# A planner's duration for a TensorE product, taken from the trace

## The chip, the cores and the metric

The kernel runs on one core of a Trainium2 chip. The core has five engines that run side by side, each with its own queue in program order: TensorE (PE, matrix products into PSUM; PEld is its weight load), VectorE (DVE), ScalarE (ACT), GpSimd (POOL) and SyncE (SP, which only issues transfers). An engine waits at a semaphore till an operand of its next instruction is ready, and what stands behind that instruction waits with it. The metric is the device time of one execution in microseconds (us); lower is better.

## The reference, cut to what matters

Two layers of a decoder trunk for 2048 prompt tokens and 8 sample tokens of width 1024, in float32:

```python
# layer 0
p = rms_norm(x) @ w_in                      # 1024 -> 3592
glu_val, glu_gate, gate_a, qkv, z, beta, a = split(p)
c = silu(layer_norm(causal_conv31(glu_val * sigmoid(glu_gate)))) * silu(gate_a)
q, k, v = silu(causal_conv4(qkv)); o = gated_delta_rule(l2(q), l2(k), v, g, beta)
x = x + concat(c, rms_norm(o) * silu(z)) @ w_out
x = x + softmax(rms_norm(x) @ wq @ k_mem.T / 16) @ v_mem @ wo
# layer 1
u, gate = split(rms_norm(x) @ w_in_odd)
x = x + ((mean_pool(u) - u) @ w_pool + b) * scale * silu(gate) @ w_out_odd
x = x + softmax(rms_norm(x) @ wq @ k_mem.T / 16) @ v_mem @ wo
y = rms_norm(x)
```

The sample tokens have memory keys and values of their own (caches of 256 rows for each token), and states for the convolutions, the delta rule and the pooling.

## The kernel before

Products are done in float32r: every operand is split into a high and a low part, and high x high, high x low and low x high are summed in a PSUM bank. An output block of 128 channels over a token tile is thus 24 products (3 pairs of parts x 8 groups of 128 input channels). Small products of side work are plain float32.

**Stages, in the order of the program.** Phase 1 makes the memory's keys and values, and then the input projection: 28 blocks of 128 channels over five token tiles (three of 512, two of 260). The blocks are ordered: four times a gate and a value block, with twelve q/k/v blocks between them, then two z blocks (2 and 3) and four sg blocks. A value block ends on DVE (`fin_val`, L222: glu <- glu, ps_mm). The long convolution (`conv31`) is 30 taps on DVE for each half of a channel block, each an operation cacc <- glu, dww, cacc over 1024 tokens, 240 in all; the short one (`conv4`) is three operations qacc on DVE after a scaled copy on ACT, and ahead of it DVE copies three columns (raw <- raw). `sample_mix` does the same for the sample tokens in many narrow steps on DVE with small products between them (ps_cs sums m_sq over the partitions; ps_ks and ps_vb belong to its delta rule, 8 times each). Phase 2 is the gated delta rule in 16 chunks (`prep`, `inv16`, `levels`, `scan`, `onorms`) beside dense products (`Fill`). Then come the output projection, the attention of layer 0, the pooling, the gated half of the odd layer, and the attention of layer 1. Beside these runs `sample_attn`, once for each layer: it reads each sample token's cached keys and values in blocks of [128, 512] over the queue of GpSimd into three places a_big, and DVE multiplies and sums each half of a block (L222: a_big <- a_big). For two such blocks there is one more load, of the query (d_sq) or the softmax weights (d_sp); this makes a round: one load of d_sq or d_sp, two blocks, four DVE operations. A layer has 32 rounds, 16 for keys and 16 for values.

**What sets the order.** Every operation is recorded through class `Flow`, which keeps a clock for each engine and for each tensor. An operation starts, by these clocks, when its engine and its operands are free, and lasts what a formula says: a product by `mm` (L160), an ACT operation by `act_cost`, a DVE operation with a per-partition factor 1/0.96 ns an element plus 130 ns (`stt`, up to L222). Dense work is a generator that yields after some four to twelve products; at each yield `pump` steps every side task whose time by the clocks has come (`item[1] <= t["pe"]`), unless DVE or ACT are by their clocks further ahead of PE than a limit (`LIM`, 1.5 to 3.8 us). `until` lets dense work stand still by the clocks till a condition holds. Some helpers choose ACT or DVE, or DVE or GpSimd, by the same clocks (`move`, `rows`, `ve`). Transfers join their queue when their data are ready by the clocks. No clock is measured: all this happens once, when the program is built, and the chip then runs each queue in the order that came out.

Of the kernel before, what the change touches and what calls it, by code (L numbers as in the profile page):

```python
# [30 lines left out]
class Pool:  # L31
    """A tile pool that notes whose place each tile takes."""
# [23 lines left out]
class Flow:  # L56
    """Engine wrappers that keep rough clocks of the engines and of the data, and the interleaving of side tasks with
    dense work by these clocks."""

    LIM = (1500.0, 3500.0, 1e9)  # L60
    # what passes from the end of an operation till another one sees its result
    VIS = {"pe": 130.0, "act": 190.0, "dve": 130.0, "pool": 110.0}

    def __init__(self, nc, tc):
        self.nc, self.tc = nc, tc
        self.rel = {}
        self.t = {"pe": 0.0, "act": 0.0, "dve": 0.0, "pool": 0.0, "sync": 0.0, "gpsimd": 0.0, "scalar": 0.0}
        self.hw = self.ring = 0.0
        self.tick, self.cold, self.cols = 0, True, 0.0
        self.cur = self.t0 = 0.0  # L70
        self.tasks = []
        # by tensor: writes and reads as (first, last partition, first, last element, time), last use, free place
        self.wr, self.rd, self.last, self.slot = {}, {}, {}, {}
        # stores that wait for their data before they join their queue: by tensor, time and arguments
        self.pend = {}
# [13 lines left out]
    def region(ap):  # L89
        a, o = ap.ap, ap.offset  # L90
        n = ap.tensor.name
        if ap.space == DRAM or a[0][0] == 0:
            # (writes to DRAM never meet earlier ones here)
            return n, -1, 1, o, o + sum((c - 1) * abs(s) for s, c in a)
# [12 lines left out]
    def ready(self, ins, outs, eng):  # L107
# [3 lines left out]
        for r in outs:  # L111
# [3 lines left out]
            # products on the same place of PSUM follow each other without a wait  # L115
# [32 lines left out]
    def pe_op(self, cost, out, lhsT, rhs):  # L148
        """the array's clock halves after a tick with too little work"""
# [10 lines left out]
    def mm(self, out, lhsT, rhs, start=True, stop=True, cost=None):  # L160
        n = fsz(rhs)
        if cost is None:
            cost = max(n, 248) * 0.422 if lhsT.dtype == F32R else max(n, 64) * 1.69
# [24 lines left out]
    def move(self, out, in_, scale=None):  # L188
        """copy on whichever of ScalarE and VectorE is free first"""
# [8 lines left out]
    def rows(self, out, in_, f):  # L198
        """out[:, h, :] = in_[:, h, :] * f[:, h], on whichever of ScalarE and VectorE ends first"""
# [7 lines left out]
    def ve(self, n, w=0.0):  # L207
        """VectorE or GpSimdE for an operation on n elements a partition, whichever ends first"""
# [55 lines left out]
    def dma(self, out, in_, eng="sync"):  # L264
        """a transfer; it joins its queue, where each waits for the ones before it, only when its data and place are ready"""
# [41 lines left out]
    def split(self, hi, lo, src, eng="dve", scale=1.0):  # L307
        """hi + lo == src, both in float32r."""
# [4 lines left out]
    def spawn(self, gen, hi=1, front=False):  # L313
        """hi: 2 what dense work waits for soon, 1 what it waits for later, 0 what may wait"""
# [34 lines left out]
    def until(self, cond):  # L349
        """dense work: let side tasks go on till cond holds"""  # L350
# [7 lines left out]
    def run(self, dense=None):  # L358
        """Alternate dense quanta (generator) with side-task steps until the dense work ends."""
# [42 lines left out]
def rsqrt(F, pool, y, x, n, tag, eng="dve"):  # L402
    """y = x ** -0.5 on a narrow float32 tile [128, n]."""
# [11 lines left out]
def token_rstd(F, C, pool, ppool, acc, n, scale, tag):  # L415
    """acc [128, n] holds partial sums; returns [128, nc] of (sum over partitions * scale + eps) ** -0.5,
    tokens on partitions."""
# [11 lines left out]
def spread(F, C, pool, ppool, r, n, tag, dg=None):  # L429
    """r [128, nc] tokens on partitions -> psum [128, n], every partition holding the row of tokens."""  # L430
# [15 lines left out]
def mm3_steps(F, out, K, w, x):  # L446
    """generator: out += (w0 + w1)^T (x0 + x1) without the product of the two low parts."""
# [21 lines left out]
class Ring:  # L469
    """Weight blocks [128, width] in two float32r parts, in n places that are taken in turn; they are loaded in parts of  # L470
    lw columns."""

    def __init__(self, F, pool, n, raw, width=1024, lw=512, tag="r"):
# [6 lines left out]
        # where the places lie, as [pool, number], and the ring that had the first ones  # L480
        self.where, self.prev = [[pool, n]], None
        # a second pool for the parts as they come, as (pool, number, up to which block)
# [6 lines left out]
    def has(self, name, i):  # L489
        """the block is in place by the clocks"""  # L490
# [10 lines left out]
    def place(self, i):  # L501
        """the pool of a block and its places"""
# [16 lines left out]
    def load(self):  # L519
        """the next part of a block"""  # L520
# [69 lines left out]
def bc(ap, n):  # L590
    """[128, k] -> [128, k, n] with the last axis repeated"""
# [4 lines left out]
def gates(F, C, cp, tp, bgp, D, st):  # L596
    """generator: per token and head beta, the cumulated log decay in its chunk, and its exponentials"""
# [16 lines left out]
    # softplus(x) = max(x, 0) + log1p(exp(-|x|))  # L614
# [8 lines left out]
    # log1p(e) = ln(u) + (e - (u - 1)) / u  # L623
# [26 lines left out]
def phase1(F, C, I, D, st, P, R, mmp, bgp, loaders, mix, hp):  # L650
    """Input projection of the even layer with its two causal convolutions. R: the weights' places; loaders: what loads
    them, and after them the weights of what follows; mix(pool): the sample tokens. The places of h are given back
    tile by tile: the first one's, hp, are taken by what follows."""
# [7 lines left out]
    def hs(t, x, k):  # L661
        """part x of h: channels k of token tile t"""
        return h0[8 * x + k] if t == 0 else ht[t][x][:, k, :]

    # (the gates of the first half, which nothing else waits for, come last)
# [22 lines left out]
    # token tiles: x -> h, beside the memory keys and values of the first layer  # L688
    with F.tile_pool(name="x1", bufs=1, side="right") as xp:
        R.more = xp, NMORE, 33  # L690
        # the last token tile's place holds the memory till its own h comes
# [37 lines left out]
        def squares():  # L729
            """adds up the squares of each token"""  # L730
# [74 lines left out]
        def ba(t, w):  # L805
            """beta and the decays before their functions, tokens on partitions"""
# [92 lines left out]
    def fin_qkv(b, t, n, ps):  # L899
        # b: 0..11  # L900
# [72 lines left out]
class Pools:  # L973
    """Pools that are opened and closed one by one."""
# [13 lines left out]
class Fill:  # L988
    """The products of the attention weights with the memory: G = w_xq^T k^T g and V w_xo of each layer and head."""
# [12 lines left out]
    def begin(self):  # L1002
        """the place of the keys and values, which come from phase 1"""
# [51 lines left out]
def phase2(F, C, I, D, st, P, fill, hp, mmp, bgp, after):  # L1055
    """Gated delta rule of the even layer, beside the products of the attention weights with the memory, in chunks of 128
    tokens, four heads at a time. It starts beside the end of phase 1, whose places it takes one after the other; what
    comes after takes its places step by step. hp: the place of the first token tile's h. Returns the dense work."""
# [12 lines left out]
    def small(tag, first, n, shape=(128, 4, 128)):  # L1071
        """one of n places that the first token tile's h had"""
# [5 lines left out]
    def room(tag, n):  # L1078
        """a place for a chunk; two of them are given back early"""
# [20 lines left out]
    # The l2 norm of k stays out of the tiles: with r = 1 / |k|, T = (1 + A)^-1 = r^-1 (1 + A')^-1 r, where  # L1100
    # A' = beta r^2 (k k^T) decay takes factors of its rows alone, and r^-1 meets the r of the next product.
    def prep(n):
# [15 lines left out]
        # decay of chunk rows i over columns j: exp(gc_i - gc_j) for j <= i  # L1118
# [69 lines left out]
    def inv16(t):  # L1188
        """inverses of the unit lower triangular blocks of 16 of two chunks, one block per partition, and their transposes"""
# [21 lines left out]
    def levels(t):  # L1211
        """blocks of 16 -> 32 -> 64 -> 128 of the transposed inverses of two chunks, which take the place of A above the
        diagonal"""
# [124 lines left out]
    def onorms(i):  # L1338
        for n in range(i, 16, 2):
# [10 lines left out]
            # |q| enters through the eps of the norm  # L1350
# [31 lines left out]
    def places():  # L1382
        """the places of phase 1, one after the other, and room for what comes after"""
# [40 lines left out]
def load_cols(F, dst, src, g, eng="sync"):  # L1424
    """columns of token group g of [128, k, NT]; the first group takes the sample tokens too"""
# [1138 lines left out]
def layout(i):  # L2564
    a = {}
# [74 lines left out]
```

## Time and profile before

| | |
|---|---|
| time, median of 3 runs | 2962.66 us (2961.9 to 2962.97) |
| span of the profiled execution | 2951.0 us, first to last instruction |
| its own time | not listed; the median lies 11.7 us above the span |
| PE, PEld busy | 2737.2 us (93%), 2500.1 us (85%) |
| DVE, ACT, POOL busy | 1987.4 us (67%), 1023.1 us (35%), 667.3 us (23%) |
| mean granted clock of PE | 0.963 |

The span is the time between the first and the last instruction; what the time has more lies around it. Busy PE is not PE at its peak, since products overlap and their ends are modelled; the distance of starts tells the pace. A float32 product of 128 columns shows as two records, a float32r product as one. The stages lie, by the first of their instructions: memory products to 183 us, projection to about 830, delta rule from there to 1254, output projection to 1430, attention of layer 0 to 1820, pooling to 2120, gated half to 2516, attention of layer 1 to the end.

### The profile page before, as it was taken

To read this page: it belongs to the slowest core of one execution; us is meant where nothing else is said; L and a number is where in the kernel's file an instruction comes from. 1 tells how busy PE (TensorE), PEld (TensorE's weight loads), DVE (VectorE), ACT (ScalarE), POOL (GpSimd) and SP (SyncE) were. 2 spreads that over 40 slices of the span, in tenths; PEclk is the share of its full clock that TensorE was granted. 3 is DMA by queue.
4 is the path that set the end of the run, shared out by engine and by line. 5 is a ranking of instruction groups with operands and counts; after the bars stand their busy time and mean duration, and the time that the engine had idled before them with its cause. 6 is when DMAs were issued, how large, how long until landed. Compare 5 with 4: busy or idle time off the path is not lost.

```text
span 2951.0 us, 52358 instructions
## 1 busy us (share of the span) xinstructions
PE 2737.2 (93%) x20075; PEld 2500.1 (85%) x20075; DVE 1987.4 (67%) x4625; ACT 1023.1 (35%) x2435; POOL 667.3 (23%) x939
## 2 busy tenths in 40 slices
PE   7899999998978678899999999899999998999997
PEld 6878888887777678789989889899999898789997
DVE  6738998988547778787665565777755445765453
ACT  5532223242245455443232234444422112432321
POOL 4301102111043455212322221111011111222210
PEclk9999999999989789899999999999999999999999
DMA  7611112123355556666654533422435556421211
GB/s 239 209 46 44 53 63 65 47 79 112 116 137 159 136 155 200 198 214 205 226 164 141 176 117 103 157 72 72 164 124 164 173 175 196 150 83 60 70 62 54
DMA packets 277723, 382.08 MB, mean 129 GB/s; under 512 B 46368, under 2 KB 176736, under 8 KB 277472
## 3 DMA queue, kind: packets, MB, share of 16 engines
q1 hardware_dynamic: 256608, 311.34, 33.6%
q0 software_dynamic: 20864, 67.39, 7.3%
q8 instruction: 158, 2.59, 0.4%
q14 instruction: 93, 0.76, 0.1%
HBM read 280.57 MB, written 96.43 MB: 128 GB/s over the span
## 4 chain that ended last, share of the span: by engine, by line
PE 35%; DMA 12%; DVE 8%; issue 4%; ACT 2%; POOL 1%; SPq 1%; DVEq 0%; POOLq 0%; ACTq 0%
PE ps_mm L165 31%; DMA a_big<-d_sp 3%; DVE a_big L222 2%; DMA a_big<-d_sq 2%; DMA w_f<-d_x 1%; PE ps_bg L165 1%; DMA rraw<-d_VW 1%; PE ps_row L165 1%; POOL w_sqb L216 1%; PE ps_pt L169 1%; DVE rlo L216 1%; DMA a_big<-in_cache_v 1%; DVE xl L216 1%; DVE w_d L216 1%; SPq L305 1%
## 5 line engine op out<-in xcount | busy, mean ns | idle before, releaser
L216 POOL TENSOR_TENSOR rlo<-rraw,rhi 128x512 fp32r<-128x512 f32 x145 | 216.9, 1505 | 610.6 <-ACT rhi L183 481.7
L222 DVE SCALAR_TENSOR_TENSOR cacc<-glu,dww,cacc 128x1024 f32<-128x1024 f32 x240 | 328.0, 1379 | 5.8 <-ACT cacc L183 1.4
L216 POOL TENSOR_TENSOR w_sqb<-w_sqb,w_sqq 128x512 f32<-128x512 f32 (+1 forms) x101 | 139.2, 1378 | 652.4 <-ACT w_sqq L183 646.5
L165 PE MATMUL ps_mm<-xh,rlo 128*128 128x256 f32 (+1 forms) x1920 | 274.4, 284 | 0.0
L165 PE MATMUL ps_mm<-xh,rhi 128*128 128x256 f32 (+1 forms) x1920 | 271.8, 284 | 2.6 <-DVE pool_sm L216 2.0
L165 PE MATMUL ps_mm<-xl,rhi 128*128 128x256 f32 (+1 forms) x1920 | 271.5, 283 | 0.0
L165 PEld LDWEIGHTS ps_mm<-xh,rhi 128*128 128x128 f32 x1920 | 248.8, 191 | 5.9 <-issue 2.2
L165 PEld LDWEIGHTS ps_mm<-xh,rlo 128*128 128x128 f32 x1920 | 249.7, 192 | 1.6
L165 PEld LDWEIGHTS ps_mm<-xl,rhi 128*128 128x128 f32 x1920 | 248.0, 190 | 2.4
L165 PE MATMUL ps_mm<-hh,rhi 128*128 128x512 f32 (+2 forms) x1152 | 217.2, 330 | 20.9 <-ACT hh L183 15.7
L165 PE MATMUL ps_mm<-hl,rhi 128*128 128x512 f32 (+2 forms) x1152 | 215.7, 330 | 0.0
L165 PEld LDWEIGHTS ps_mm<-hh,rhi 128*128 128x128 f32 x1152 | 178.6, 192 | 42.9 <-ACT hh L183 16.1
L165 PE MATMUL ps_mm<-hh,rlo 128*128 128x512 f32 (+2 forms) x1152 | 214.7, 329 | 0.0
L216 DVE TENSOR_TENSOR w_y<-ps_mm,w_y 128x256 f32<-128x256 f32 (+1 forms) x248 | 103.1, 420 | 159.3 <-PE ps_mm L165 155.1
L222 DVE SCALAR_TENSOR_TENSOR a_big<-a_big 128x256 f32<-128x256 f32 x256 | 104.0, 444 | 148.7 <-DMA a_big<-d_sp 80.9
L183 ACT ACTIVATE rhi<-rraw 128x512 fp32r<-128x512 f32 x233 | 143.1, 628 | 164.4 <-DMA rraw<-d_VW 36.3
L165 PEld LDWEIGHTS ps_mm<-hl,rhi 128*128 128x128 f32 x1152 | 178.1, 192 | 17.6
L165 PEld LDWEIGHTS ps_mm<-hh,rlo 128*128 128x128 f32 x1152 | 177.0, 192 | 18.9 <-issue 1.0
L165 PE MATMUL ps_mm<-mh,rhi 128*128 128x256 f32 (+1 forms) x1152 | 170.1, 288 | 8.6 <-ACT mh L183 8.6
L165 PE MATMUL ps_mm<-ml,rhi 128*128 128x256 f32 (+1 forms) x1152 | 170.7, 290 | 3.1 <-DVE ml L216 3.1
L165 PE MATMUL ps_mm<-mh,rlo 128*128 128x256 f32 (+1 forms) x1152 | 163.6, 283 | 0.0
L165 PEld LDWEIGHTS ps_mm<-mh,rhi 128*128 128x128 f32 x1152 | 153.5, 195 | 11.2 <-ACT mh L183 9.5
(426 smaller groups left out, 5360.1 us busy)
## 6 DMA issues: line engine op xcount, KB each, us to landing
w_f<-d_x SPq DMA_DIRECT2D x60, 512.0 KB
d_x<-w_y SPq DMA_DIRECT2D x44, 512.0 KB
w_y<-d_x SPq DMA_DIRECT2D x44, 512.0 KB
a_big<-in_cache_k POOLq DMA_DIRECT2D x64, 256.0 KB, 4.1
a_big<-in_cache_v POOLq DMA_DIRECT2D x64, 256.0 KB, 4.1
rraw<-in_w_in SPq DMA_DIRECT2D x56, 256.0 KB
d_qkv<-so SPq DMA_DIRECT2D x48, 256.0 KB
rraw<-in_w_xk SPq DMA_DIRECT2D x32, 256.0 KB
```

The source lines that it names most:

```text
L165: self.nc.tensor.matmul(out, lhsT, rhs, start=start, stop=stop)
L169: self.nc.tensor.transpose(out, in_, ident)
L183: self.nc.scalar.activation(out=out, in_=in_, func=func, scale=scale, **kw)
L216: self._e(eng).tensor_tensor(out=out, in0=a, in1=b, op=op)
L222: self._e(eng).scalar_tensor_tensor(out=out, in0=a, scalar=s, in1=b, op0=op0, op1=op1, **kw)
L305: getattr(self.nc, eng).dma_start(out=out, in_=in_)
```

## The change

One formula in `mm` is different, that of the PE clock's step for a product of n columns. In the first case it goes from max(n, 248) x 0.422 to max(n, 240) x 0.426 + 9 ns (float32r; for 256 columns from 108.0 to 118.1, for 512 from 216.1 to 227.1), in the second from max(n, 64) x 1.69 to max(n, 64) x 1.68 + 10 ns (float32; for 128 columns from 216.3 to 225.0). The rest of the difference between the files takes out comments, and shifts line numbers after L162 by one.

```diff
     def mm(self, out, lhsT, rhs, start=True, stop=True, cost=None):
         n = fsz(rhs)
         if cost is None:
-            cost = max(n, 248) * 0.422 if lhsT.dtype == F32R else max(n, 64) * 1.69
+
+            cost = max(n, 240) * 0.426 + 9.0 if lhsT.dtype == F32R else max(n, 64) * 1.68 + 10.0
         self.pe_op(cost, out, lhsT, rhs)
         self.nc.tensor.matmul(out, lhsT, rhs, start=start, stop=stop)
```

The formula is read when the program is built, so the products themselves stay as they are; what stands beside them moves. On PE, at the end of the projection, the first small product of the sample's mixing (ps_cs, which sums m_sq) stands before the change in the second token tile of the first sg block (hh_245 and hl_246 are this tile's high and low parts; hh_240 and hl_241 are those of the third tile):

```order
L165 MATMUL ps_mm<-h_218,rlo 128x512
L165 MATMUL ps_mm<-hh_245,rhi 128x512 x8
L165 MATMUL ps_cs<-m_sq,ones 128x64
L165 MATMUL ps_mm<-hl_246,rhi 128x512 x8
L165 MATMUL ps_mm<-hh_245,rlo 128x512 x8
L165 MATMUL ps_mm<-hh_240,rhi 128x512 x8
```

With the change PE has it in the third tile of the block before, z block 3:

```order
L166 MATMUL ps_mm<-hh_245,rlo 128x512 x8
L166 MATMUL ps_mm<-hh_240,rhi 128x512 x8
L166 MATMUL ps_mm<-hl_241,rhi 128x512 x4
L166 MATMUL ps_cs<-m_sq,ones 128x64
L166 MATMUL ps_mm<-hl_241,rhi 128x512 x4
L166 MATMUL ps_mm<-hh_240,rlo 128x512 x8
```

It moved ahead of 92 dense products: 44 of 512 columns and 48 of 260. On DVE, around the last value block of the projection (its five glu operations, one for each token tile), before the change:

```order
L222 SCALAR_TENSOR_TENSOR qacc<-raw,scw,qacc 128x512 x3
L222 SCALAR_TENSOR_TENSOR cacc<-glu,dww,cacc 128x1024 x4
L222 SCALAR_TENSOR_TENSOR glu<-glu,ps_mm 128x512
L222 SCALAR_TENSOR_TENSOR cacc<-glu,dww,cacc 128x1024 x8
L222 SCALAR_TENSOR_TENSOR glu<-glu,ps_mm 128x512
L222 SCALAR_TENSOR_TENSOR cacc<-glu,dww,cacc 128x1024 x8
L222 SCALAR_TENSOR_TENSOR glu<-glu,ps_mm 128x512
L222 SCALAR_TENSOR_TENSOR cacc<-glu,dww,cacc 128x1024 x4
```

And with the change, at the same place on DVE:

```order
L223 SCALAR_TENSOR_TENSOR qacc<-raw,scw,qacc 128x512 x3
L223 SCALAR_TENSOR_TENSOR cacc<-glu,dww,cacc 128x1024 x6
L223 SCALAR_TENSOR_TENSOR glu<-glu,ps_mm 128x512
L223 SCALAR_TENSOR_TENSOR cacc<-glu,dww,cacc 128x1024 x6
L223 SCALAR_TENSOR_TENSOR glu<-glu,ps_mm 128x512
L223 SCALAR_TENSOR_TENSOR cacc<-glu,dww,cacc 128x1024 x10
L223 SCALAR_TENSOR_TENSOR glu<-glu,ps_mm 128x512
L223 SCALAR_TENSOR_TENSOR cacc<-glu,dww,cacc 128x1024 x4
```

Counted from the start of DVE's order, 144 taps stand ahead of the first of these glu operations before and 158 with the change, 168 and 182 ahead of the fifth, and 226 and 236 ahead of m_sq. On DVE at the end of layer 1's sample attention (the reads show as a_big,a_oT<-a_big; w_y, w_d, ml, rlo and xl are dense work's), before:

```order
L216 TENSOR_TENSOR w_d<-w_d,w_c 128x256
L216 TENSOR_TENSOR xl<-w_f,xh 128x1024
L222 SCALAR_TENSOR_TENSOR a_big,a_oT<-a_big 128x256 x2
L216 TENSOR_TENSOR ml<-w_d,mh 128x256
L216 TENSOR_TENSOR w_y_26913<-ps_mm,w_y_26913 128x256 x3
L216 TENSOR_TENSOR rlo<-rraw,rhi 128x512 x3
L222 SCALAR_TENSOR_TENSOR a_big,a_oT<-a_big 128x256 x2
L216 TENSOR_TENSOR w_y_26913<-ps_mm,w_y_26913 128x256
```

The same end of the reads on DVE with the change:

```order
L217 TENSOR_TENSOR w_y_26419<-ps_mm,w_y_26419 128x256 x3
L223 SCALAR_TENSOR_TENSOR a_big,a_oT<-a_big 128x256 x4
L217 TENSOR_TENSOR w_y_26419<-ps_mm,w_y_26419 128x256
L217 TENSOR_TENSOR w_y_26542<-ps_mm,w_y_26542 128x256
L223 SCALAR_TENSOR_TENSOR a_big,a_oT<-a_big 128x256 x2
L217 TENSOR_TENSOR w_y_26542<-ps_mm,w_y_26542 128x256
L223 SCALAR_TENSOR_TENSOR a_big,a_oT<-a_big 128x256 x2
L217 TENSOR_TENSOR w_y_26542<-ps_mm,w_y_26542 128x256 x2
```

The reads stand closer together: from the first to the last one of a layer PE's order has 1714 products before and 1540 with the change in layer 0, and 1982 and 1705 in layer 1.

## Rows read from the trace of the kernel before

**Rows 1.** The page's head: the span, and PE's busy time.

```profile
span 2951.0 us, 52358 instructions
PE 2737.2 (93%) x20075; PEld 2500.1 (85%) x20075; DVE 1987.4 (67%) x4625; ACT 1023.1 (35%) x2435; POOL 667.3 (23%) x939
```

**Rows 2.** Windows of the projection: length, busy time (instructions) by engine, clock, DMA.

```profile
core 0: us, PE busy (x) PEld busy (x) DVE busy (x) ACT busy (x) POOL busy (x), PEclk, DMA share, GB/s
...
300.00:400.00 100.00, 97.20 (x514) 84.54 (x513) 94.11 (x92) 25.20 (x48) 15.48 (x11) 0.98 0.17 60
400.00:500.00 100.00, 100.00 (x554) 87.57 (x553) 93.32 (x93) 26.02 (x54) 15.81 (x11) 1.00 0.15 51
...
sum 465.00, PE 451.69 PEld 392.34 DVE 431.89 ACT 134.69 POOL 80.60; mean PE 90.34 PEld 78.47 DVE 86.38 ACT 26.94 POOL 16.12
```

**Rows 3.** DVE's groups, 247 to 712 us: count, busy us, mean ns, idle before.

```profile
L222 DVE SCALAR_TENSOR_TENSOR cacc<-glu,dww,cacc 128x1024 f32<-128x1024 f32 x212 | 290.1, 1383 | 3.8
L222 DVE SCALAR_TENSOR_TENSOR qacc<-raw,scw,qacc 128x512 f32<-128x512 f32 x144 | 117.0, 812 | 28.7 <-ACT qacc L183 25.3
```

**Rows 4.** DVE's waits, 247 to 712 us, and one of them in the timeline.

```profile
DVE qacc L222 <- ACT qacc L183: 25.3, 27, 3.2
...
608.14 1.54 DVE L222 SCALAR_TENSOR_TENSOR qacc<-raw,scw,qacc 128x512 f32<-128x512 f32 x2 [0.85 <-ACT qacc L183]
```

**Rows 5.** PE's waits, 200 to 776 us: total us, times, longest.

```profile
PE ps_cs L165 <- DVE m_sq L216: 6.3, 1, 6.3
PE ps_mm L165 <- DVE glu L222: 5.2, 2, 2.8
```

**Rows 6.** Windows of the delta rule (with PE's longest wait) and both sample attentions.

```profile
811.00:1254.00 443.00, 355.84 (x4024) 320.38 (x4023) 315.91 (x966) 229.53 (x752) 182.41 (x367) 0.85 0.59 164
...
1430.00:1706.00 276.00, 271.99 (x1756) 245.66 (x1756) 159.33 (x543) 74.76 (x165) 81.05 (x118) 1.00 0.54 174
2247.00:2516.00 269.00, 244.55 (x1963) 241.35 (x1961) 133.34 (x453) 54.11 (x111) 51.54 (x95) 0.96 0.59 184
...
PE ps_bg L165 <- DVE S L222: 8.8, 5, 4.0
```

**Rows 7.** PE's pace: timeline from 655 to 665 us, window of 256-column products.

```profile
654.67 3.83 PE L165 MATMUL ps_mm<-h,rhi 128*128 128x512 f32 x16
...
663.78 1.52 PE L165 MATMUL ps_mm<-hh,rlo 128*128 128x512 f32 x6
...
1991.90:2065.70 73.80, 73.80 (x617) 73.70 (x616) 52.29 (x102) 32.93 (x68) 13.06 (x11) 1.00 0.22 72
```

**Rows 8.** PE's timeline at the end of the projection.

```profile
689.54 1.98 PE L165 MATMUL ps_mm<-hl,rhi 128*128 128x512 f32 x8
...
712.66 0.69 PE L165 MATMUL ps_cs<-m_sq,ones 128*128 128x64 f32 x2 [6.27 <-DVE m_sq L216]
...
775.66 1.10 PE L165 MATMUL ps_vb<-m_dd,ones 128*128 128x512 f32 x2
```

**Rows 9.** Timeline of layer 1's rounds: first and last read, one round's loads.

```profile
2247.01 0.42 DVE L222 SCALAR_TENSOR_TENSOR a_big<-a_big 128x256 f32<-128x256 f32 x1
...
2516.05 0.42 DVE L222 SCALAR_TENSOR_TENSOR a_big<-a_big 128x256 f32<-128x256 f32 x1
...
2453.47 0.54 POOL L305 DMA_DIRECT2D a_big<-d_sp  x1 [2.12 <-DVE a_big L222]
...
2460.39 0.54 POOL L305 DMA_DIRECT2D a_big<-d_sp  x1 [0.49 <-DVE a_big L222]
...
2458.29 0.43 DVE L222 SCALAR_TENSOR_TENSOR a_big<-a_big 128x256 f32<-128x256 f32 x1 [2.90 <-DMA a_big<-d_sp]
```

**Rows 10.** PE's and DVE's waits, 2247 to 2518 us.

```profile
PE ps_bc L165 <- DVE w_sqq L229: 13.5, 4, 4.0
PE ps_mm L165 <- ACT mh L183: 8.6, 4, 6.8
...
DVE a_big L222 <- DMA a_big<-d_sq: 38.4, 13, 4.1
```

## The prediction

> **What bounds the kernel now.** I began with the page's head: TensorE (PE) is busy 2737.2 of 2951.0 us [rows 1], so there are little over 200 us to win, and what decides is where PE waits and for whom. Then the windows view, stage by stage. In the input projection, from 247 to 712 us, PE and VectorE (DVE) are full at the same time: PE 451.7 and DVE 431.9 of 465 us [rows 2]. Of the 33.1 us that DVE is idle there, 25.3 are 27 waits for ScalarE (ACT) ahead of the short convolution [rows 4]; 8 us are left. The reader is to see that DVE has no room in this stage: its work there is the 240 taps of the long convolution, 1383 ns each, and the short convolutions at 812 ns an operation [rows 3]. PE pays for that as far as 776 us with 6.3 us before the product ps_cs, which waits for DVE's m_sq, and 5.2 us for glu [rows 5]. The delta-rule stage loses more, 87 of 443 us, with PE's clock granted at 0.85 on average; the sample's attention of layer 0 loses 4 of 276 us; that of layer 1 24 of 269 us [rows 6], in part because DVE stands in its queue before operands that a DMA still brings (38.4 us for d_sq alone) [rows 10].
>
> **What the change does, step by step.** The work stays the same; some operations change between ACT, DVE and GpSimd (ACT has 19 instructions more, since it does four where DVE does one). What moves is the place of side work among the products. The planner's PE clock goes from 216.1 to 227.1 ns for 512 columns and from 108.0 to 118.1 for 256. The trace has 40 products of 512 columns between 654.67 and 663.78 us, 228 ns each, and 617 of 256 in 73.8 us, 119.6 ns each [rows 7]. So the new PE clock is right. But the other clocks stay: a tap counts 1024/0.96 + 130 = 1197 ns and takes 1383; an operation of the short convolution counts 663 and takes 812 [rows 3]. Before, PE was planned 5 to 10% too fast and DVE 13 to 18% too fast, and the two mistakes nearly cancelled. Now PE is right and DVE still too fast, so more DVE work is put ahead of each product than DVE can do in that time.
>
> The Trainium skill would see the old number as the right one: TensorE: Matmul & The Clock Gate, section Back-to-back issue gap, gives N/2.4 + 2.5 ns at full clock, 109 ns for 256 columns; the trace shows 119.6. With the page's figures the 92 products of the next part would be an estimated 14.8 us instead of 16.0, and the sum 1.2 us lower.
>
> *Projection, DVE's side.* Counted in the two orders, the taps that stand ahead of a given operation grow by 2 at the second channel block's first glu, 8 at the third's, and 14 at the twentieth and last glu; 10 are left at m_sq (236 instead of 226). DVE has been full since 247 us, so it ends m_sq later by 10 x 1383 ns = 13.8 us; ps_cs, at 712.66 us before, can start at 726.5. The lower bound is that DVE wins back its 25.3 us of waits: 701.2. I take 726.5, since each such wait (0.85 us [rows 4]) is for ACT's copy, which itself waits for the small copy that DVE makes just ahead of it: both orders have that pair, and DVE being late doesn't end it.
>
> *Projection, PE's side.* ps_cs now stands 92 products earlier, behind the fourth hl product of token tile 2 of z block 3. PE passed this place at 690.4 us before (the hl row at 689.54 plus four products) [rows 8]. PE works in order, so wherever it waits on the way, at glu or at ps_cs, it is 726.5 - 690.4 = 36.1 us late there. The kernel before then loses its own 6.3 us before ps_cs, which the new one has behind it: 29.8 us remain. It is the same as 13.8 us of taps and 16.0 us for the 92 products (690.4 to 706.4, where the old wait began), which used to cover DVE and now come after. From ps_cs to the end of the sample's mixing (775.66) [rows 8] little can be won back: some 2 us, as 2 taps instead of 12 are left between the steps of the mixing. I take 28. Bounds: with ps_cs at 701.2 the lateness is 10.8 - 6.3 = 4 us; at the high end 30 and some 3 us for a lower clock after the long wait (0.98 was granted in the stretch with waits, 1.00 where there were none [rows 2]).
>
> *Delta rule.* The first products of its 16 scan steps shift by at most 7 us of PE work, to both sides, and by under 1.5 us in the last seven. I price it at 0. The bounds of +9 and -9 are the longest kind of wait there, 8.8 us in all, doubled or gone [rows 6].
>
> *Sample attention.* Between the first and the last read of the cached keys and values 1714 products stood in layer 0 and 1982 in layer 1; now 1540 and 1705, because the chain's latencies are counted in a PE clock that runs slower. One round (a load of the query or weights, two reads) can't be shorter than about 6.9 us: its load was issued at 2453.47, the operation that needs it started at 2458.29, and the next round's load was issued at 2460.39 [rows 9]. Layer 1 has 32 rounds, 31.75 from the first read to the last: at least 219 us, for 1705 x 0.12 = 204.6 us of products; before they took 269.0 us (2247.01 to 2516.05), 8.5 us a round. The 277 products that leave the chain cost 33.2 us behind it. If rounds shrink to 6.9 us: 219 + 33.2 = 252, a gain of 17. If they stay at 8.5: 269 + 33.2 = 302, a loss of 33. I take the middle, +8. Layer 0: PE's 272 us shrink to 272 x 1540/1714 = 244, 7.7 us a round, still above 6.9: hidden in the mean, not in each round. Bounds 0 and 8 (the rounds that fall short), I take 4.
>
> **The sum.** 28 + 0 + 4 + 8 = 40 us on the profiled span of 2951.0: 2991. The runs' median, 2962.66, is 11.7 us above this span; with that left as it is the time is 3003 us.
>
> **Rivals.** *No change that can be measured* (within 0.2%, 6 us, about what a measurement of this kernel can tell): DVE takes up the taps. For it: 33 us of idle time in the projection. Against: 25.3 of them are bound to the pair above. Then 4 + 0 + 0 + 0: 2967 us; it decides at the point where less than about 2 us of the 13.8 remain and the chain costs nothing.
> *Faster, by the delta rule.* Its place is 811 to 1254 us, with the largest loss in the kernel. If the new order kept PE's clock up there, the 355.8 us of busy PE at 0.85 could shrink by up to 53 us: 3003 - 53 = 2950. It must bring more than 46 us to decide, that is nearly the whole clock. Against: the scan steps keep their places to 7 us.
> *Slower still.* The rounds of layer 1 keep their 8.5 us (+33 for +8) and the projection takes its high end (+5): 3033 us. For it: each round of layer 1 already has DVE waiting for d_sp or d_sq, and PE waits behind it for w_sqq (13.5 us) and mh (8.6) [rows 10].
>
> **Chances and range.** The forecast (2980 to 3025) 0.70, slower still 0.12, no change 0.10, faster 0.08. So slower by over 0.2%: 0.82; within: 0.10; faster: 0.08. The range of 2975 to 3030 leaves out the last two cases and part of slower still, about 2 in 10. Its low end is the forecast with the projection at 15 us and the chains at 0 or a little below; its high end has layer 1 at about +33.
>
> **What the changed profile would show.** ps_cs on m_sq starts at 722 to 730 us; PE's waits for glu and m_sq together grow from 11.5 to 30 us or more; DVE stays over 92% busy from 300 us till then, still with some 25 us of waits for ACT's qacc; the last ps_vb of the mixing is over by about 780, and the sg products that used to stand ahead of it come after. The scan ends some 28 us later, with the delta rule's length unchanged to 10 us. In layer 1 the time from the first to the last read is below 269 us, but by less than 33.
> The prediction is wrong if DVE reaches m_sq before 715 us (the ACT waits shrink, or the taps are hidden), if PE's delay at 776 us is won back by 1254 us, or if the delta rule moves by tens of us.

## The result: slower by 3.2%, over twice what was forecast

The changed kernel takes 3054.39 us (median of 4 runs, 3051.66 to 3059.36) against 2962.28: a ratio of 1.0321, 95% interval 1.0307 to 1.0334. The direction was forecast, the size was not: +92 us on the median (+102.4 on the profiled spans) for a predicted +40, outside the range. The two differ because the trace of the kernel before is one of its shorter executions: in all other runs the time lies 1.7 to 2.1 us above the span, which puts this one at some 2953 us (an estimate), and not 11.7 us of work around the span. So sums against this trace hold up to 10 us that no change made.

The page's head of the changed kernel, to be held against [rows 1]:

```profile
span 3053.4 us, 52352 instructions
PE 2757.8 (90%) x20075; PEld 2518.5 (82%) x20075; DVE 1968.8 (64%) x4616; ACT 1028.9 (34%) x2454; POOL 654.5 (21%) x935
```

The same products are 20 us longer in PE's busy time, since more of them run at the lower of TensorE's two clocks (mean granted clock 0.953 for 0.963), and the other 82 us are idle. Windows of the changed kernel, with the columns of [rows 2]: two of the projection, the projection to ps_cs, the delta rule, and the two sample attentions from the first to the last use of a cache read:

```profile
300.00:400.00 100.00, 95.38 (x504) 82.78 (x503) 94.14 (x92) 26.05 (x52) 16.66 (x12) 0.98 0.17 56
400.00:500.00 100.00, 94.29 (x495) 81.68 (x494) 95.06 (x90) 24.88 (x48) 16.60 (x13) 0.97 0.16 55
247.00:725.00 478.00, 450.21 (x2394) 389.98 (x2392) 448.48 (x461) 133.65 (x254) 71.07 (x54) 0.98 0.20 64
...
820.00:1277.00 457.00, 356.34 (x4077) 322.52 (x4075) 306.85 (x979) 242.16 (x803) 179.93 (x364) 0.88 0.59 162
1460.00:1733.00 273.00, 244.57 (x1540) 222.92 (x1539) 143.89 (x504) 63.81 (x136) 78.17 (x114) 0.94 0.54 171
2338.00:2580.00 242.00, 215.04 (x1696) 212.50 (x1695) 113.37 (x418) 39.02 (x80) 50.32 (x94) 0.92 0.59 179
```

The reader is to see the fifth row. In layer 0, PE was busy 272 of 276 us at the full clock [rows 6]; now 28 of 273 us are idle, and the clock is 0.94. The stage is nearly as long as before though about 220 instructions have left it, and those come behind it. Layer 1, in the last row, did get shorter. PE's waits in the projection, in the out-projection (1272 to 1454 us) and in layer 0:

```profile
PE ps_mm L166 <- DVE glu L223: 10.1, 4, 4.5
PE ps_mm L166 <- ACT raw L184: 9.7, 6, 3.5
PE ps_cs L166 <- issue: 8.0, 1, 8.0
...
PE ps_mean L166 <- DVE w_sqa L244: 8.3, 6, 2.4
PE ps_ss L166 <- POOL w_sqa L217: 7.6, 4, 5.2
PE ps_bg L170 <- ACT o L184: 5.5, 1, 5.5
...
PE ps_ss L166 <- POOL w_sqa L217: 26.9, 5, 7.6
```

ps_ss takes the sum of squares that a norm needs; GpSimd adds these squares (w_sqb, then w_sqa), and ACT makes them (w_sqq). In layer 0 before (1430 to 1706 us), the same wait was small, and no other was longer:

```profile
PE ps_ss L165 <- POOL w_sqa L216: 2.2, 3, 1.2
```

**A ledger.** To place the loss I gave each product the same weight in both orders (228 ns for 512 columns, 119.6 for 256, one weight for each f32 shape) and read from the traces when PE had done the same sum of work. How much later the changed kernel reaches what the kernel before has done at a given time: 7.3 us at 247, 23.8 at 820, 23.4 at 1254, 42.3 at 1420, 87.2 at 1750, 93.4 at 2240, 97.5 at 2600, and 102.4 at 2900, which is the difference of the spans. So layer 0 costs 45 us, the out-projection that follows the scan 19, the projection 16.5 and the start, ahead of it, 7. The delta rule costs nothing, layer 1 costs 4. The mark of 820 us is read just ahead of a wait that the kernel before has there, since no work is done in it; read at its other end, it is 18.8:

```profile
819.18 0.72 PE L165 MATMUL ps_mm<-hh,rhi 128*128 128x260 f32 x4
824.68 1.09 PE L169 MATMUL ps_bg<-ident,q 128*128 128x128 f32 x4 [4.78 <-DMA q<-d_qkv]
```

The ledger has one trace for each kernel, and executions of one kernel lie 5 to 22 us apart in their time, so differences of some 5 us mean little.

### The profile page after: what moved, and what is told of

The parts are those of the page before. It is cut to its first block, busy times and chain, and to the rows that moved or that the text cites. A ratio compares the mean times of both kernels' runs of the same rounds, so it can differ in the third digit from the quotient of the medians.

```text
span 3053.4 us, 52352 instructions
## 1 busy us (share of the span) xinstructions
PE 2757.8 (90%) x20075; PEld 2518.5 (82%) x20075; DVE 1968.8 (64%) x4616; ACT 1028.9 (34%) x2454; POOL 654.5 (21%) x935
## 4 chain that ended last, share of the span: by engine, by line
PE 40%; DVE 25%; DMA 17%; issue 7%; ACT 5%; POOL 3%; SPq 2%; DVEq 0%; ACTq 0%; POOLq 0%
PE ps_mm L166 34%; DVE cacc L223 8%; DVE qacc L223 3%; DMA a_big<-d_sp 3%; SPq L306 2%; PE ps_bg L166 2%; DMA w_f<-d_x 2%; DMA a_big<-d_sq 2%; DVE a_big L223 2%; DMA a_big<-in_cache_k 1%; POOL w_sqb L217 1%; DVE rlo L217 1%; DMA rraw<-d_G 1%; DMA d_VW<-gv 1%; DVE w_d L217 1%
## 5 line engine op out<-in xcount | busy, mean ns | idle before, releaser
L217 POOL TENSOR_TENSOR rlo<-rraw,rhi 128x512 fp32r<-128x512 f32 x139 | 203.4, 1473 | 601.7 <-ACT rhi L184 417.1
L166 PE MATMUL ps_mm<-mh,rhi 128*128 128x256 f32 (+1 forms) x1152 | 170.6, 289 | 18.1 <-ACT mh L184 18.1
```

Source lines behind the costliest of these rows:

```text
L166: self.nc.tensor.matmul(out, lhsT, rhs, start=start, stop=stop)
L217: self._e(eng).tensor_tensor(out=out, in0=a, in1=b, op=op)
```

## The experiments

Fourteen kernels ran, each beside the kernel before on the same chip. In the short diffs, `old` is a switch in `Flow`: where it is set, products are priced as before. The first four take the loss apart by place.

**e1: the new durations as far as the end of the projection.**

```diff
+        F.old = True
         delta()
```

> New product durations as far as the end of the input projection and the mixing, the old ones from the delta rule on. Theory A (the loss is a sum of places, each with its own cause): the part before 820 us keeps its own loss, 20 to 25 us (ps_cs at 725 us, last ps_vb near 780), and nothing more is lost in layer 0 or 1: 2980 to 2992 us. Theory B (the order of before is a lucky one, and any other order loses wherever it differs): the later stages also lose, 3010 us or more.

3007.13 us, ratio 1.0169 (1.0150 to 1.0189): between the two theories. By the ledger it is 29 us late at 820, 12 of them from the start, where 20 to 25 were expected, and loses 7 in layer 0. But it loses 14 between 820 and 1420, where its prices are the old ones. A loss there need not be made by the new price there: it can come with another state of the plan at the end of the projection.

**e2: new only in layer 0's cache reads; e3: old only there.** The switch is turned by `sample_attn`, ahead of its first read and behind its last.

```diff
+    if l == 0:
+        F.old = False        # e3: True
     sc = t([128, 2, 32], "sc")
...
+    if l == 0:
+        F.old = True         # e3: False
     yield
```

> Old durations everywhere but between the first and the last cache read of the sample's attention in layer 0, where the new ones hold: 1508 products stand in that chain instead of 1762 (231.7 us of PE work instead of 270.4). Theory A (the chain is bound by its own rounds at 8.6 us and does not get shorter when it is given fewer products): it still takes 270 to 280 us, PE waits there 25 us or more, and the time is 2995 to 3003 us. The prediction's own step (rounds shrink with their products): 2965 to 2970 us.

> The reverse: new durations everywhere but in the cache reads of layer 0, which get 1766 products (262.4 us of PE work). Theory A: the chain of layer 0 takes about 278 us with PE waiting under 10 us in it, and the time falls by 30 to 40 us from the changed kernel's, to 3014 to 3025 us. If the loss of layer 0 was inherited from the lateness of earlier stages instead: still 3040 us or more.

e2 takes 2978.05 us, ratio 1.0073 (1.0053 to 1.0093); e3 3017.92, ratio 1.0216 (1.0188 to 1.0244), some 36 us below the changed kernel. The windows of layer 0, first of e2, then of e3:

```profile
1435.00:1695.00 260.00, 243.24 (x1525) 219.62 (x1524) 149.37 (x509) 65.85 (x144) 76.28 (x115) 0.95 0.55 173
```

```profile
1458.00:1733.00 275.00, 265.99 (x1762) 244.37 (x1761) 157.30 (x536) 70.03 (x149) 79.62 (x118) 0.98 0.56 178
```

e3 gives the products back and the stage is no longer for them: 275 us with 1762 instructions against 273 with 1540. That is the clearest row of the study. e2 lies between its two theories: with about 230 instructions fewer than before its chain is some 16 us shorter, where theory A expected nothing, and it loses 28 us by the ledger, where the prediction's step expected 4. So the chain does shrink, but by less than half of the 39 us of PE work that the plan took out of it (270.4 less 231.7).

**e4: the changed kernel, with GpSimd's reads planned to land 0.8 us later.**

```diff
-        self.mark(ri, ro, "dma", self.ring, self.ring + 900)
+        self.mark(ri, ro, "dma", self.ring, self.ring + (1700 if eng == "gpsimd" else 900))
```

> The changed kernel, and a transfer issued by GpSimd is planned to land 0.8 us later, so that the plan's 3.3 us from issue to use become 4.1 us, the median of the trace of before. The chains get 1770 products (layer 0) and 2143 (layer 1). Theory A: layer 0 waits under 10 us again (-30 to -36 us), layer 1 takes about 275 us for 261 us of work (-10 to -22 us): 2996 to 3014 us. If the number of products per round is not what makes layer 0 wait: PE still waits for w_sqa by 20 us or more there, and 3035 us or more.

3015.07 us, ratio 1.0201 (1.0169 to 1.0233), just above what was expected: layer 0 loses 12 us by the ledger instead of 45, layer 1 gains 9, and PE's wait for w_sqa in layer 0 falls to 10.3 us. A price of a product and a latency of a read are two ways to set the same thing, how many products stand in a round.

**e5: the changed kernel with slower taps; e6: with e4's edit too.** `dep` was a parameter that `stt` didn't use.

```diff
-        c = 68 if isinstance(s, float) else 130
+        c = (68 if isinstance(s, float) else 130) + dep
...
-            F.stt(acc, g[:, o + i:o + i + 1024], C.dww[:, b, i:i + 1], acc, ALU.mult, ALU.add)
+            F.stt(acc, g[:, o + i:o + i + 1024], C.dww[:, b, i:i + 1], acc, ALU.mult, ALU.add, dep=91)
```

(and dep=54 in the short convolution)

> The changed kernel, and an operation of the long convolution is planned 91 ns longer, one of the short convolution 54 ns longer, as the trace of before has them. Counted in the order, 226 taps stand ahead of m_sq again (236 in the changed kernel, 226 before), and ps_cs stands at product 3811 (3711; 3803 before). Theory A (the projection lost because the plan's DVE was too fast beside a right PE): PE waits under 8 us for glu, raw and m_sq between 250 and 776 us, ps_cs at 715 to 722 us, and 15 to 25 us come back: 3029 to 3040 us, or 3012 to 3025 if the seam after the scan (some 18 us) comes back with it. If DVE's planned speed is not what matters there: no change, 3050 us or more.

> Both corrections: slower taps and reads that land 0.8 us later. Theory A (the plan needs clocks that agree with each other, and each corrected clock gives back its own place): the gains add, 3015 us less 15 to 40: 2975 to 3000 us; layer 0 loses under 15 us, the projection under 10. Theory B (before's order is a lucky one): still above 3005 us.

e5: 3041.90 us, ratio 1.0296 (1.0262 to 1.0330), an interval that overlaps the changed kernel's; 12.5 us came back where 15 to 25 were expected. Its waits in the projection are nearly those of before again [rows 5], though above the 8 us that theory A allowed:

```profile
PE ps_cs L166 <- DVE m_sq L217: 6.0, 1, 6.0
PE ps_mm L166 <- DVE glu L223: 3.5, 3, 2.6
PE ps_mm L166 <- ACT raw L184: 2.6, 3, 1.5
```

By the ledger the projection's loss is gone (1 us won instead of 16 lost), and 10 of these 17 us are lost again between 820 and 1420. e6 takes 3015.16 us, ratio 1.0201 (1.0177 to 1.0225), no better than e4 alone: a miss. It enters the delta rule 15 us earlier than e4 and leaves the out-projection 5 us later.

**e7: the kernel before with e4's edit.**

> The kernel before with only the later landing of GpSimd's reads: the chains get 1832 products (1762 before) and 2206 (1963), 10 and 45 us of PE work more. Theory A: layer 0 stays as it is, layer 1's chain takes 285 to 295 us for 281.8 us of work and loses 8 to 20 us less than before: 2943 to 2955 us, faster than before. If what the chain gains is lost behind it, or its rounds stretch with the products: 2955 to 2965 us.

2949.65 us, ratio 0.9975 (0.9962 to 0.9988): a little faster, and by the ledger from layer 1 (9.5 us), as expected. That layer's chain took 313 us, though, not 285 to 295.

**e8 and e12: the opposite step, products planned 5 and 10% shorter than before; e11: e8 with e4's edit.**

```diff
-            cost = max(n, 240) * 0.426 + 9.0 if lhsT.dtype == F32R else max(n, 64) * 1.68 + 10.0
+            cost = max(n, 248) * 0.401 if lhsT.dtype == F32R else max(n, 64) * 1.605
```

(e12: 0.38 and 1.521)

> The kernel before with every product planned 5% shorter still (0.401 for 0.422, 1.605 for 1.69), the opposite step: 214 taps ahead of m_sq, 1782 and 2148 products in the chains. Theory A (each place has a direction: fewer products per round lose, more do not): no loss in the chains (layer 1 loses 10 us less), DVE idles more in the projection, 10 to 20 us of taps then come late behind it: 2945 to 2975 us. Theory B (any other order than before's loses, to both sides): 2990 us or more.

> Products planned 5% shorter and reads landing 0.8 us later, the two that were faster alone: the chains get 1972 and 2114 products. If the two gains are in different places: 2930 to 2940 us. If they are one gain (more products per round of the chains), nothing is added to the shorter products' 2943: 2940 to 2950 us.

> Every product planned 10% shorter than before (0.38, 1.521): 212 taps ahead of m_sq, 1916 and 2148 products in the chains. If a shorter product goes on gaining: 2925 to 2940 us. If the best lies between: 2943 to 2975 us, with the loss where side work comes late (the delta rule starts later, and layer 1's chain ends nearer the end of the program).

e8 takes 2943.39 us, ratio 0.9953 (0.9932 to 0.9975), e11 2943.72, ratio 0.9961 (0.9948 to 0.9974), e12 2998.12, ratio 1.0137 (1.0114 to 1.0159). With the price of 512 columns at 195, 205, 216 and 227 ns the time is 2998, 2943, 2959 and 3054 us: theory B falls, as one step away from the old price is faster, and the best of the four is 205, some 10% under the true duration. e8 is just under its range, e11 says that the two gains are one, and e12 is a miss: it is above both of its ranges.

**e9: only the fp32r formula is new.**

> Only the fp32r formula is new, the f32 formula (which prices most products of the delta rule) stays that of before. The order has ps_cs at the same place (3711, behind 236 taps) and 1556 and 1695 products in the chains, as in the changed kernel. Theory A (projection and layer 0, both fp32r, make the loss): 3040 to 3060 us. If the f32 products of the delta rule had a part: lower by 15 us or more.

3052.08 us, ratio 1.0321 (1.0298 to 1.0345), as theory A has it: within the noise the fp32r formula is the whole loss.

**e10: the kernel before with slower taps.**

> The kernel before with the slower taps alone (91 and 54 ns more each): 220 taps ahead of m_sq instead of 226, ps_cs at product 3839 instead of 3803. Theory A says of the projection that PE waits for glu, raw and m_sq fall from 13.9 to under 4 us there; the rest as before: 2940 to 2960 us. If the two errors had cancelled best as they were, DVE now falls idle and its taps come late behind the projection: slower than before, 2962 to 2985 us.

2963.64 us, ratio 1.0021 (1.0004 to 1.0037). The time lies in the range of the second case, that the errors had cancelled. In the projection it does what theory A expected:

```profile
PE ps_mm L165 <- DVE glu L222: 1.4, 1, 1.4
PE ps_mm L165 <- ACT raw L183: 1.4, 1, 1.4
PE ps_cs L165 <- DVE m_sq L216: 0.4, 1, 0.4
```

It reaches 820 us some 23 us ahead of the kernel before, and at 1420 it is 5 us behind. e8 goes the same way, from 40 us ahead at 820 to 6 ahead at 1420. Their windows of the delta rule, from 820 us to the last scan step, e8 first:

```profile
820.00:1241.00 421.00, 320.21 (x3776) 289.36 (x3774) 297.91 (x935) 212.17 (x712) 167.97 (x353) 0.83 0.60 162
```

```profile
820.00:1257.00 437.00, 334.49 (x3852) 298.30 (x3851) 308.48 (x954) 220.84 (x725) 182.10 (x364) 0.83 0.60 160
```

The rule's length is not that of PE's work: PE is idle for over 100 us in each. The scan's first update of S is 23 us (e8) and 28 us (e10) later than before, and from the first update to the last it takes 319 us in e8 and 331 in e10 for 356 before. So what PE gains ahead of the scan comes back only in part. That this is because work which used to be done beside the projection is still ahead of the scan, and that the scan then sets the pace, is argued from PE's idle time and not shown by a run.

**e13 and e14: the norms' squares added on DVE**, in the changed kernel and in that of before, so that GpSimd's queue holds the reads alone.

```diff
-def square_sum(F, W, x, n, acc=None, last=True, eng="pool"):
+def square_sum(F, W, x, n, acc=None, last=True, eng="dve"):
...
-            acc = square_sum(F, W, y[h], 256, acc, h == 1, "pool" if g < NG - 1 else "dve")
+            acc = square_sum(F, W, y[h], 256, acc, h == 1, "dve")
```

They were made for this piece of the changed kernel's timeline, GpSimd in layer 0:

```profile
1515.04 0.54 POOL L306 DMA_DIRECT2D a_big<-in_cache_k  x1
1524.43 1.37 POOL L217 TENSOR_TENSOR w_sqb<-w_sqb,w_sqq 128x512 f32<-128x512 f32 x1 [8.85 <-ACT w_sqq L184]
1525.74 0.56 POOL L306 DMA_DIRECT2D a_big<-in_cache_k  x1
...
1526.82 0.54 POOL L306 DMA_DIRECT2D a_big<-in_cache_k  x1
1538.00 1.37 POOL L217 TENSOR_TENSOR w_sqb<-w_sqb,w_sqq 128x512 f32<-128x512 f32 x1 [10.64 <-ACT w_sqq L184]
```

The read of 1525.74 starts at once when the add ahead of it is done: it waited for the queue at the end, not for its buffer. The add waits for ACT, where the square at 1537.29 stands behind the softmax's operations, which wait for DVE, which is in the chain again. So reads, squares and softmax wait for each other around a ring of queues in this piece, and PE's ps_ss at 1543.16 waits for all of it (7.64 us).

> The changed kernel with the adds of the norms' squares (w_sqb, w_sqa) on VectorE instead of GpSimd, whose queue then holds the cache reads alone; the plan puts 1476 products (222.6 us of PE work) into layer 0's chain. If layer 0's rounds are long because the reads stand behind the squares in GpSimd's queue (8.6 us a round for a shortest of 6.9): 235 to 250 us for the chain, and the loss of layer 0 falls from 45 to 13 to 28 us: 3022 to 3040 us. If the rounds are as long for another reason: the chain stays at 265 to 275 us, loses 45 to 52 us, and the time is 3050 to 3065 us.

> The same move in the kernel before; the plan then puts 1588 products (241 us of PE work) into layer 0's chain, 29 us less than before. If the queue makes the rounds long: a chain of 245 to 258 us, and 2958 to 2975 us. If not: the chain stays near 275 us, and 2980 to 2995 us.

e13: 3044.51 us, ratio 1.0279 (1.0246 to 1.0313); e14: 2967.99, ratio 1.0036 (1.0024 to 1.0049). The windows of layer 0, e13 first:

```profile
1482.00:1735.00 253.00, 232.33 (x1457) 209.66 (x1456) 144.14 (x512) 62.64 (x133) 50.20 (x94) 0.95 0.57 181
```

```profile
1434.00:1693.00 259.00, 245.38 (x1581) 222.18 (x1580) 152.18 (x532) 69.43 (x150) 50.33 (x94) 0.98 0.57 178
```

e13's 32 rounds take 7.9 us each instead of 8.5, and its layer 0 loses 31 us by the ledger instead of 45. So GpSimd's queue is at most a part of what makes the rounds long: the time lies half-way between the expectations. How large a part is not shown, since e13 also takes 83 instructions more out of the chain, and e2, in which squares and reads share the queue, has rounds of 8.1 us and loses 28 us with nearly as many instructions as the changed kernel. Its time was expected at 3022 to 3040 and is above: it also lost 8 us more than the changed kernel between 820 and 1420, and 5 at the start. e14's time is within the first case, its chain of 259 us just above it.

**The ledger of all**, in us late against the kernel before (rounded; the same order ran with 3 to 5 us of spread at the start; 820 is read just ahead of the wait named above):

| kernel | start, to 247 | projection, to 820 | delta rule, out-projection, to 1420 | layer 0, to 1750 | rest | sum |
|---|---|---|---|---|---|---|
| changed | 7 | 16 | 19 | 45 | 15 | 102 |
| e1 new in the projection | 12 | 17 | 14 | 7 | 4 | 54 |
| e2 new in layer 0 | 0 | 1 | 4 | 28 | -3 | 30 |
| e3 old in layer 0 | 10 | 16 | 13 | 11 | 12 | 63 |
| e4 reads later | 9 | 17 | 15 | 12 | 1 | 54 |
| e5 taps slower | 9 | -1 | 29 | 32 | 15 | 83 |
| e6 both | 11 | 0 | 35 | 15 | 5 | 66 |
| e7 before, reads later | -4 | -2 | 6 | 0 | -4 | -5 |
| e8 5% shorter | -6 | -34 | 33 | 0 | -2 | -9 |
| e9 fp32r alone | 10 | 16 | 21 | 35 | 16 | 98 |
| e10 before, taps slower | 1 | -23 | 28 | 2 | 4 | 11 |
| e11 5% shorter, reads later | -5 | -34 | 31 | -7 | 8 | -7 |
| e12 10% shorter | 5 | -24 | 64 | -3 | 1 | 43 |
| e13 squares on DVE | 13 | 17 | 27 | 31 | 10 | 98 |
| e14 before, squares on DVE | 0 | -1 | 7 | 16 | -5 | 18 |

## Why the prediction went wrong

The sum was 28 (projection) + 0 (delta rule) + 4 (layer 0) + 8 (layer 1); the ledger has 16.5 + 0 + 45 + 4, and 37 in places that had no term: 19 in the out-projection, 7 at the start, 6 between 1750 and 2240 us and 5 after 2600.

**The step that failed is that of layer 0**: "PE's 272 us shrink to 272 x 1540/1714 = 244, 7.7 us a round, still above 6.9: hidden in the mean". The count was about right (about 220 instructions fewer by the windows, 174 products counted). The floor was not. 6.9 us was one round, of layer 1, and not a lower limit: layer 0 of the same trace has one of 5.8 us, from the issue of one d_sq load to the next:

```profile
1534.87 0.54 POOL L305 DMA_DIRECT2D a_big<-d_sq  x1 [4.76 <-DVE a_big L222]
...
1540.63 0.54 POOL L305 DMA_DIRECT2D a_big<-d_sq  x1 [0.16 <-issue]
```

Nor does a single round tell what a chain of 32 does; that is the mean round, which in layer 0 was 8.5 us in the changed kernel and 8.1 in e2, against 8.6 before. Before, PE's work and the chain were equally long (272 and 276 us), so taking work out could only help as far as the rounds shrank, and they hardly did: 273 us instead of the 244 forecast. The products that left came behind the chain at their full price, and PE waited five times in it, for 3.7 to 7.6 us; at each of these waits the granted clock fell to the lower of its two levels, to 0.94 in the mean. I read "4 us lost" [rows 6] as room; it only said that PE hid the chain, not by how much. e3 shows it: given its products back, the stage is 2 us longer, and the loss falls to 11 us; in e4 it is 10 us longer, and the loss falls to 12:

```profile
1465.00:1748.00 283.00, 270.10 (x1761) 245.46 (x1761) 154.91 (x541) 72.77 (x157) 79.67 (x118) 0.98 0.55 173
```

How the step's own effect (28 us in e2, 32 in e5, 35 in e9) becomes 45 in the changed kernel is open: GpSimd's queue may have a part of it (e13), and which dense steps fall beside which rounds another, but no run separates them.

**Projection: place and mechanism right, size too high.** ps_cs and the last ps_vb of the changed kernel's timeline answer to [rows 8]; behind them stand DVE's first tap and m_sq, of the kernel before and of the changed one:

```profile
716.01 1.07 PE L166 MATMUL ps_mm<-hl,rhi 128*128 128x512 f32 x4
725.06 0.66 PE L166 MATMUL ps_cs<-m_sq,ones 128*128 128x64 f32 x2 [7.99 <-issue]
...
775.23 1.10 PE L166 MATMUL ps_vb<-m_dd,ones 128*128 128x512 f32 x2
```

```profile
225.87 1.28 DVE L222 SCALAR_TENSOR_TENSOR cacc<-glu,dww,cacc 128x1024 f32<-128x1024 f32 x1 [1.37 <-ACT cacc L183]
...
712.38 0.23 DVE L216 TENSOR_TENSOR m_sq<-m_s 128x64 f32<-128x64 f32 x1
```

```profile
233.17 1.28 DVE L223 SCALAR_TENSOR_TENSOR cacc<-glu,dww,cacc 128x1024 f32<-128x1024 f32 x1 [1.37 <-ACT cacc L184]
...
724.74 0.22 DVE L217 TENSOR_TENSOR m_sq<-m_s 128x64 f32<-128x64 f32 x1
```

726.5 was predicted, and the place is the one named, behind four hl products. (The wait is put down to issue; m_sq ended at 724.96.) But that the time agrees is luck in part: DVE's first tap was already 7.3 us late, from the start, which had no term, and from there to m_sq the ten taps more cost 5.1 us (491.6 for 486.5), not 13.8. DVE was busy 448 of 478 us. The waits for ACT's qacc fell by 4 us, to 21.3 in 25, so DVE won back little of its idle time; where the rest of the 13.8 us went I have not separated. PE's waits for glu and m_sq are 18.1 us, where 30 or more were predicted, and 9.7 for ACT's raw, which I hadn't named. The ledger shows 37.5 us at 700 us, but 7.3 of them are from the start, 6.3 the kernel before still had ahead of it, and after ps_cs more than the assumed 2 us came back: 16.5 of the 28 remain at 820.

**The reason given for it was half right.** "A tap counts 1197 ns and takes 1383" left out that the plan lets a result be read only 130 ns later (`VIS`), so that a chain of taps is planned at 1327 ns each. DVE was planned 7% too fast, with the 35 ns between two taps, not 13 to 18%. By the ledger that 7% is what matters there, since e5's correction of 91 ns undoes the projection's loss. But "the two mistakes nearly cancelled" doesn't hold as a rule: in e10, where the taps alone are corrected, the projection gets better by 23 us, though 28 are lost behind it. The sentence on the Trainium skill in the prediction carries no term of the sum; its page, TensorE: Matmul & The Clock Gate, section Back-to-back issue gap, gives N/2.4 + 2.5 ns as the gap of an isolated product, so it does not make the old price the right one for a stream of products that each load weights.

**Delta rule: right, its end was not.** It costs nothing by the ledger, as priced. The first operation of the last scan step's update of S is at 1276.25 us, 22.6 us later than before. The out-projection behind it had no term and lost 19: PE waits for sums and for the scan's last output (ps_mean, ps_ss, ps_bg, 21 us). Between 820 and 1420 every kernel with another price of products or taps ahead of that loses 13 us or more, e1 too, in which the prices there are the old ones. Why the order of before loses least there is open.

**Layer 1: right.** Its chain went from 270.3 us to 240.8 (first to last read issued), and loses 4 us for a predicted 8; rounds of 7.6 us are near the middle that I took between 6.9 and 8.5, which was a compromise and not a reading. Why the rounds shrink here and hardly in layer 0 is open. **The start** was not looked at: PE waits 17.7 us there for sums of squares and their inverse roots where it waited 12.3.

The rivals had the sign of the changes right: neither the delta rule's clock (0.88 for 0.85) nor the idle time of DVE paid for anything. The slower one named layer 1 and should have named layer 0. None of the three signs of being wrong came true, as they watched the projection and the delta rule alone.

## What to carry to other kernels

A number in a plan can be wrong in the way that the rest of the plan needs: here a product's price sets how many products cover each step of a latency chain, and the true price leaves too few (e3, e4); set such a price by trying it on both sides (e8, e12). Where PE and a chain of waits are equally long, a profile without waits is a knee and not room: take the chain's floor from the mean round, in that stage, and ask what stands in the queues between its steps. And what a stage gains can be given back in the next (e8, e10), so read a gain at the end of the program and not where it is made.

## What the hardware showed that I had not expected

A tap of the long convolution has one short duration or a much longer one, and nothing between. Of the changed kernel's 240 taps, 219 took 1.28 us on average (none over 1.29), the other 21 took 1.99 to 2.40. Each of the long ones overlaps an operation of GpSimd on 512 elements. So do 16 of the short ones, by at most 1.09 us, so that overlap alone does not make a tap long. The first row below is two taps alone, the last one tap that met them:

```profile
411.30 2.60 DVE L223 SCALAR_TENSOR_TENSOR cacc<-glu,dww,cacc 128x1024 f32<-128x1024 f32 x2
...
422.36 2.98 POOL L217 TENSOR_TENSOR rlo<-rraw,rhi 128x512 fp32r<-128x512 f32 x2 [20.32 <-ACT rhi L184]
424.03 2.40 DVE L223 SCALAR_TENSOR_TENSOR cacc<-glu,dww,cacc 128x1024 f32<-128x1024 f32 x1
```

So the mean of 1383 ns in [rows 3] was a mixture (in the trace before 216 taps of 1.28 us and 24 of 1.98 to 2.40), and the plan's price of a tap can be right for 9 taps in 10 and still 7% short. The Trainium skill says in Trainium Architecture — The Big Picture, section What this means for kernel authors, that DVE and GpSimd share a port under an exclusive lock, not by a split of bandwidth; that no tap lies between the two agrees with that, though no run here took the overlap away.
